# Squares moved to GpSimd, a first chunk in quarters, a last product in halves: one change to a two-layer hybrid block

## The chip, the cores and the metric

One core of one Trainium2 chip runs the whole program. The metric is the device time of one execution in microseconds (us); the median of several runs counts. The engines are TensorE (PE, its weight loads PEld), VectorE (DVE), ScalarE (ACT), GpSimd (POOL) and SyncE (SP), which issues nearly all DMAs here.

## What is computed

Two layers act on x of 256 tokens by 2048 features, float32. The first layer mixes a retention branch and a sparse attention branch, the second a convolution branch and a dilated attention branch. Each begins with a root-mean-square norm and a wide projection, and ends with an output product that is added to x:

```
def rms_norm(x, gain):
    y = x * rsqrt(mean(x * x, axis=-1) + 1e-6)
    return y * gain

def even_layer(x, ...):
    h = rms_norm(x, norm_g) @ w_in          # 2048 x 7704
    ...                                     # retention, sparse attention, gates
    return x + concatenate([a_out, b_out], -1) @ w_out

def odd_layer(x, ...):
    h = rms_norm(x, norm_g) @ w_in          # 2048 x 8192
    ...                                     # convolution, dilated attention, gates
    return x + concatenate([c_out, d_out], -1) @ w_out
```

The change touches the sum of squares and the first two projections at the very start, and the last output product at the very end.

## The kernel before

The kernel computes the products with three matmuls each: a float32 operand is split into a rounded part and a remainder, and hi x hi, hi x lo and lo x hi are added in PSUM. For weights the parts are `wh` (a cast on ScalarE, L109) and `wl` (`raw` minus `wh` on VectorE, L110), made by `prep`; a chunk of 512 rows of a weight comes in two halves of two k-tiles (128 rows) each, 128x1024 numbers a half. The pools of `raw`, `wh` and `wl` have five buffers each, so a load waits for a `wl` made earlier, and a cast for matmuls that are through with an earlier half. For x the parts are `xh` (ScalarE, L191) and `xl` (VectorE, L192), made by `norm_block` from `xT`, the transposed input, with the norm's gain multiplied in; the norm's factor per token is applied to the results later.

At the start `project_both` (L246) runs two projections side by side over four chunks c of x: for each c first the product into `mm` (q = 0), then that into `both` (q = 1). In the first chunk of q = 0 each k-tile is loaded, cast and split by itself (`cut`), with the load of the x k-tile between; all other chunks go by halves. `square_block` (L196) squares one block of four k-tiles of x on ScalarE (L201) and folds it on VectorE (L202, then L204 or L206, and L207) into `sqs`; `token_squares` (L213) sums that over the partitions on TensorE, and `token_rstd` makes the norm's factor with a power on GpSimd (L221). GpSimd has nothing but small settings of memory before that. `xtok` (L742), x by tokens for the residual sum, is loaded by SP into the place of `xT`, so its load waits until all reads of `xT` are done.

A planner in the compiler puts each engine's instructions into one fixed order by priority and estimated times; `high_priority` lifts weights and evacuations. In a run each engine keeps its order and waits on semaphores. So the order in which the engines work is not always that of the source lines.

At the end `project` (L114) computes the last output product, four times 512 columns: per chunk and half, for both token tiles t, six matmuls of 512 columns each. After a token tile's last matmul `evac_out` (L959) adds the residual on VectorE (L965) and stores (L966); for the very last tile it does so in two halves of 256 columns, one after the other.

Of the kernel before, what the change touches and what calls it, by code (L numbers as in the profile page):

```python
# [16 lines left out]
AF = mybir.ActivationFunctionType  # L17
ALU = mybir.AluOpType
# [18 lines left out]
HPO = 2000  # L37
# [22 lines left out]
def hybrid_kernel(ctx: ExitStack, tc: tile.TileContext, a: dict, out: bass.AP):  # L60
    nc = tc.nc
# [28 lines left out]
    def prep(src, n, cut=None, half=None):  # L90

        with tc.high_priority(offset=HPO):
            parts = []
            for hf in range(2):
                raw = wp.tile([128, 2, 512], F32, name="raw", tag="raw")
                wh = wp.tile([128, 2, 512], F32R, name="wh", tag="wh")
                wl = wp.tile([128, 2, 512], F32R, name="wl", tag="wl")
                if cut:
                    for k in range(2):
                        nc.sync.dma_start(raw[:, k, :n], src[:, 2 * hf + k, :])  # L100
                        cut(2 * hf + k)
                else:
                    nc.sync.dma_start(raw[:, :, :n], src[:, 2 * hf:2 * hf + 2, :])
                    if half:
                        half(hf)
                for k in ((0, 1), (1, 2)) if cut else ((0, 2),):
                    k = slice(*k)
                    r = raw[:, k, :n]
                    nc.scalar.copy(wh[:, k, :n], r)  # L109
                    nc.vector.tensor_sub(wl[:, k, :n], r, wh[:, k, :n].bitcast(F32))  # L110
                parts.append((wh, wl))
        return parts

    def project(src, n, lhs, evac, korder=None, lazy=None, extra=None, cut=None,  # L114
                flip=False):

        nch = src.shape[0]
        acc = [ps.tile([128, 512], F32, name=f"mm{t}", tag="mm", bufs=MMB) for t in range(2)]  # L120
        order = korder or list(range(nch))
        for i, c in enumerate(order):
            if lazy:
                lazy(c)
            parts = prep(src[c], n, cut=(lambda k: cut(c, k)) if cut and i < 3 else None)
            xh, xl = lhs[c]
            for hf in range(2):
                wh, wl = parts[hf]
                for t in range(2):
                    for j in range(2):  # L130
                        for k in range(2):
                            kk = 2 * hf + k
                            first = i == 0 and kk == 0
                            last = i == nch - 1 and kk == 3
                            if flip:
                                cs = slice((2 * t + j) * 128, (2 * t + j) * 128 + 128)
                                o = acc[t][:, j * S:j * S + S]
                                kw = dict(skip_group_check=True)
                                nc.tensor.matmul(o, wh[:, k, cs], xh[:, kk, :], start=first and j == 0, stop=False, **kw)  # L139
                                nc.tensor.matmul(o, wl[:, k, cs], xh[:, kk, :], start=False, stop=False, **kw)  # L140
                                nc.tensor.matmul(o, wh[:, k, cs], xl[:, kk, :], start=False, stop=last, **kw)  # L141
                            elif j == 0:
                                ts = slice(t * 128, t * 128 + 128)
                                o = acc[t][:, :n]
                                nc.tensor.matmul(o, xh[:, kk, ts], wh[:, k, :n], start=first, stop=False)  # L145
                                nc.tensor.matmul(o, xh[:, kk, ts], wl[:, k, :n], start=False, stop=False)  # L146
                                nc.tensor.matmul(o, xl[:, kk, ts], wh[:, k, :n], start=False, stop=last)  # L147
                    if i == nch - 1 and hf == 1:
                        with tc.high_priority(offset=HPO):
                            evac(t, acc[t])  # L150
            for f in (extra or {}).get(i, ()):
                f()
# [26 lines left out]
    xT = res.tile([128, KT, S], F32, name="xT", tag="x")  # L179
    sqs = [None]  # L180
# [14 lines left out]

    def square_block(b):  # L196

        if b == 0:
            sqs[0] = hp.tile([128, S], F32, name="sqs", tag="h")
        sq = hp.tile([128, 4, S], F32, name="sqb", tag="h")  # L200
        nc.scalar.activation(sq, xT[:, 4 * b:4 * b + 4, :], AF.Square)  # L201
        nc.vector.tensor_add(sq[:, 0:2, :], sq[:, 0:2, :], sq[:, 2:4, :])  # L202
        if b == 0:
            nc.vector.tensor_add(sqs[0], sq[:, 0, :], sq[:, 1, :])  # L204
        else:
            nc.vector.tensor_add(sq[:, 0, :], sq[:, 0, :], sq[:, 1, :])  # L206
            nc.vector.tensor_add(sqs[0], sqs[0], sq[:, 0, :])  # L207

    def token_squares(tot):

# [27 lines left out]
    lhs = []  # L238
# [4 lines left out]
    def load_x(b, k0=0, k1=4):  # L243
        nc.sync.dma_start(xT[:, 4 * b + k0:4 * b + k1, :], a["xT"][:, 4 * b + k0:4 * b + k1, :])

    def project_both(srcs, accs, evacs):  # L246

        nch = srcs[0].shape[0]
        for c in range(nch):
            for q in range(2):  # L250
                begin = c == 0 and q == 0
                parts = prep(srcs[q][c], 512, cut=(lambda k: load_x(0, k, k + 1)) if begin else None,
                             half=(lambda hf: load_x(c, 2 * hf, 2 * hf + 2)) if c and q == 0 else None)
                with tc.high_priority(offset=HPO):
                    if begin:
                        lhs.append(norm_block(0, evn, first=True))
                    elif q == 0:
                        lhs.append(norm_block(c, evn))
                if q == 0 and c == nch - 1:
                    square_block(c)  # L260
                xh, xl = lhs[c]
                for hf in range(2):
                    if q == 0 and c == nch - 1 and hf == 1:
                        rstd.append(token_rstd(token_squares(sqs[0]), "rstd1"))
                    wh, wl = parts[hf]
                    for t, k in [(t, k) for k in range(2) for t in range(2)] if begin else \
                            [(t, k) for t in range(2) for k in range(2)]:
                        kk = 2 * hf + k
                        last = c == nch - 1 and kk == 3
                        ts = slice(t * 128, t * 128 + 128)  # L270
                        o = accs[q][t]
                        nc.tensor.matmul(o, xh[:, kk, ts], wh[:, k, :], start=c == 0 and kk == 0, stop=False)  # L272
                        nc.tensor.matmul(o, xh[:, kk, ts], wl[:, k, :], start=False, stop=False)  # L273
                        nc.tensor.matmul(o, xl[:, kk, ts], wh[:, k, :], start=False, stop=last)  # L274
                        if last:
                            with tc.high_priority(offset=HPO):
                                evacs[q](t, o)
                if q == 0 and c < nch - 1:
                    square_block(c)
# [64 lines left out]
    for i, pos in enumerate((posk, posv)):  # L344
# [7 lines left out]
        for c in range(2):  # L352
            b = hp.tile([128, 16, 64], F32R, name=f"bhl{i}{c}", tag="h")
            nc.gpsimd.memset(b.bitcast(F32), 0.0)
            v = blk[:, 16 * c:16 * c + 16, :]
# [125 lines left out]
    for i in range(2):  # L481
        h = htile(f"nq{i}")
        if i == 0:
            def evac_gates(t, p, h=h):
# [4 lines left out]
                    extra={0: [k_turned, compress(1, 1)], 1: [k_normed], 2: [k_done, v_turned], 3: [v_done]})  # L489
# [14 lines left out]
    for h in range(8):  # L504
        for t in range(2):
            o = pc[:, (t * 8 + h) * 32:(t * 8 + h) * 32 + 32]
            k = kcT[:, h // 4, :, :].rearrange("p a n -> p (a n)")
# [26 lines left out]
    for h in range(8):  # L534
        g, r = h // 4, slice(32 * (h % 4), 32 * (h % 4) + 32)
        for n, src in enumerate((pch, pch, pcl)):
            v = src[r].rearrange("p (t g) k -> p t g k", t=2)[:, :, g, :]
# [137 lines left out]
    for hf in range(2):  # L675
# [5 lines left out]
        v = htile(f"rv{hf}")  # L681
# [55 lines left out]
    lhs = mix  # L737
# [3 lines left out]
    xtok = res.tile([128, 2, D], F32, name="xtok", tag="x")  # L741
# [29 lines left out]
    lhs = nxt  # L771
# [46 lines left out]
    apad, acc = [], []  # L818
# [77 lines left out]
    for p_ in range(3):  # L896
        v = htile(f"dv{p_}")
# [51 lines left out]
    mix, turns = [], []  # L949
    for i in range(3):  # L950
        extra = take(range(4))
# [5 lines left out]
    lhs = mix  # L957

    def evac_out(n):  # L959
        def f(t, p):  # L960
            w = 256 if n == 3 and t else 512
            for c in range(0, 512, w):
                k = 512 * n + c
                v = xtok[:, t, k:k + w]
                nc.vector.tensor_add(v, p[:, c:c + w], v)  # L965
                nc.sync.dma_start(out[t, :, k:k + w], v)  # L966
        return f

    for n in range(4):
        project(a["owo"][n], 512, lhs, evac_out(n), extra={} if n else {0: [turns[2]]})  # L970


def _constants():
# [87 lines left out]
```

## Time and profile before

| | |
|---|---|
| median of 3 runs | 939.23 us (939.16 to 939.35) |
| the profiled execution | 939.11 us |
| its span | 937.3 us |
| TensorE busy | 930.5 us (99%) |
| VectorE busy | 642.3 us (69%) |
| ScalarE busy | 507.5 us (54%) |
| GpSimd busy | 71.1 us (8%) |
| granted clock of TensorE | 0.999 of full speed |

The profile is one execution; its times count from the start of the span, and 1.8 us of the measured time lie around the span. In the chain of work that ended last TensorE has 97%. A mean over the span says little about the two places that the change touches, so the rows below are of these places, and of places where the engines in question worked side by side in a comparable way.

### The profile page before, as it was taken

Reading aid. Unit: us, or ns where it says so; the run is one execution under the profiler, and the core shown is the slowest. Engines: PE = TensorE matmul, PEld = TensorE weight load, DVE = VectorE, ACT = ScalarE, POOL = GpSimd, SP = SyncE. Lnnn points to the kernel's source line nnn. Section 1 sums busy time; section 2 is a strip of 40 time slices with the busy share of each in tenths; the row PEclk is TensorE's granted clock in tenths of the full one; section 3 lists DMA queues with packets and bytes.
Section 4 is the critical chain, followed back from the end, with each engine's and each line's share of the span. In section 5 each row is a group of like instructions: output and inputs, shape, how many; then the busy total and the mean of one; then the engine's idle time right before and its main releaser. Section 6 shows DMA issues by size and latency. Waiting matters only on the chain.

```text
span 937.3 us, 13151 instructions
## 1 busy us (share of the span) xinstructions
PE 930.5 (99%) x4949; PEld 798.7 (85%) x4949; DVE 642.3 (69%) x947; ACT 507.5 (54%) x762; POOL 71.1 (8%) x72
## 2 busy tenths in 40 slices
PE   8999999999999999999999999999999999999998
PEld 7889989989998888888888888888888888888886
DVE  7687657875654564654464499999999998546552
ACT  7566656655544544544465353556665444797341
POOL 0111100320220100000000000000000002200000
PEclk9999999999999999999999999999999999999999
DMA  9967754354446555555555555555555656434461
GB/s 332 348 204 220 249 189 149 120 176 156 152 164 207 161 170 182 185 195 181 196 185 168 192 180 180 190 190 190 185 186 185 202 197 189 148 116 157 149 226 53
DMA packets 52512, 173.48 MB, mean 185 GB/s; under 512 B 5728, under 2 KB 10720, under 8 KB 52320
## 3 DMA queue, kind: packets, MB, share of 16 engines
q1 hardware_dynamic: 52304, 172.63, 55.8%
q8 instruction: 39, 0.64, 0.3%
q14 instruction: 25, 0.20, 0.1%
q10 hardware_dynamic: 144, 0.01, 0.0%
HBM read 170.52 MB, written 2.10 MB: 184 GB/s over the span
## 4 chain that ended last, share of the span: by engine, by line
PE 97%; DMA 1%; DVE 1%; ACT 0%; issue 0%; SPq 0%; DVEq 0%
PE mm L145 25%; PE mm L147 25%; PE mm L146 25%; PE mm L139 3%; PE mm L141 3%; PE mm L140 3%; PE tr L315 3%; DMA raw<-in_ew 1%; PE dpo L931 1%; PE dsc L911 1%; PE cmph L377 1%; PE tr L579 1%; PE both L273 1%; PE both L274 0%; PE both L272 0%; PE mm L274 0%
## 5 line engine op out<-in xcount | busy, mean ns | idle before, releaser
L110 DVE TENSOR_TENSOR wl<-raw,wh 128x1024 fp32r<-128x1024 f32 (+2 forms) x322 | 385.1, 1202 | 215.0 <-ACT wh L109 208.1
L109 ACT CAST wh<-raw 128x1024 fp32r<-128x1024 f32 (+2 forms) x322 | 328.4, 1025 | 343.5 <-PE mm L147 252.1
L146 PE MATMUL mm<-wl,xh 128*128 128x512 f32 (+1 forms) x1056 | 406.4, 385 | 0.0
L145 PE MATMUL mm<-wh,xh 128*128 128x512 f32 (+1 forms) x1056 | 406.1, 386 | 0.0
L147 PE MATMUL mm<-wh,xl 128*128 128x512 f32 (+1 forms) x1056 | 403.3, 384 | 0.0
L147 PEld LDWEIGHTS mm<-wh,xl 128*128 128x128 f32 x1056 | 198.4, 188 | 38.1
L145 PEld LDWEIGHTS mm<-wh,xh 128*128 128x128 f32 x1056 | 198.2, 188 | 37.9 <-issue 0.2
L146 PEld LDWEIGHTS mm<-wl,xh 128*128 128x128 f32 x1056 | 198.5, 188 | 37.4
L801 DVE SCALAR_TENSOR_TENSOR cps<-apad,pb,cps 128x256 f32<-128x256 f32 x240 | 116.8, 487 | 5.3
L139 PE MATMUL mm<-xh,wh 128*128 128x256 f32 x256 | 73.2, 287 | 0.0
L140 PE MATMUL mm<-xh,wl 128*128 128x256 f32 x256 | 72.8, 285 | 0.0
L141 PE MATMUL mm<-xl,wh 128*128 128x256 f32 x256 | 72.5, 283 | 0.0
L140 PEld LDWEIGHTS mm<-xh,wl 128*128 128x128 f32 x256 | 49.0, 192 | 0.0
L141 PEld LDWEIGHTS mm<-xl,wh 128*128 128x128 f32 x256 | 49.0, 191 | 0.0
L139 PEld LDWEIGHTS mm<-xh,wh 128*128 128x128 f32 x256 | 48.9, 191 | 0.0
L567 ACT ACTIVATE p<-p,nm 128x128 f32<-128x128 f32 (+1 forms) x32 | 14.2, 445 | 15.5 <-DVE nm L563 15.4
L643 POOL TENSOR_TENSOR rot<-rot,pb 128x512 f32<-128x512 f32 x8 | 11.2, 1406 | 78.3 <-ACT rot L641 78.0
L299 ACT ACTIVATE sq<-d 128x128 f32<-128x128 f32 x48 | 14.3, 303 | 0.3
L273 PE MATMUL both<-wl,xh 128*128 128x512 f32 x32 | 12.8, 401 | 1.2 <-DVE wl L110 1.2
L644 POOL TENSOR_TENSOR rT<-rT,rot 128x512 f32<-128x512 f32 x8 | 13.1, 1660 | 0.0
L272 PE MATMUL both<-wh,xh 128*128 128x512 f32 x32 | 12.6, 394 | 0.0
L274 PE MATMUL both<-wh,xl 128*128 128x512 f32 x32 | 12.5, 390 | 0.0
(294 smaller groups left out, 724.0 us busy)
## 6 DMA issues: line engine op xcount, KB each, us to landing
raw<-in_ow SPq DMA_DIRECT2D x128, 512.0 KB, 4.5
raw<-in_ew SPq DMA_DIRECT2D x110, 512.0 KB, 4.2
raw<-in_ewo SPq DMA_DIRECT2D x32, 512.0 KB, 4.0
raw<-in_owo SPq DMA_DIRECT2D x24, 512.0 KB, 4.1
raw<-in_ewn SPq DMA_DIRECT2D x16, 268.0 KB, 3.5
xtok<-in_xtok SPq DMA_DIRECT2D x1, 2048.0 KB, 8.3
raw<-in_w1k SPq DMA_DIRECT2D x4, 512.0 KB, 6.4
raw<-in_w1v SPq DMA_DIRECT2D x4, 512.0 KB, 4.2
```

Source lines behind the costliest of these rows:

```text
L109: nc.scalar.copy(wh[:, k, :n], r)
L110: nc.vector.tensor_sub(wl[:, k, :n], r, wh[:, k, :n].bitcast(F32))
L139: nc.tensor.matmul(o, wh[:, k, cs], xh[:, kk, :], start=first and j == 0, stop=False, **kw)
L140: nc.tensor.matmul(o, wl[:, k, cs], xh[:, kk, :], start=False, stop=False, **kw)
L141: nc.tensor.matmul(o, wh[:, k, cs], xl[:, kk, :], start=False, stop=last, **kw)
L145: nc.tensor.matmul(o, xh[:, kk, ts], wh[:, k, :n], start=first, stop=False)
L146: nc.tensor.matmul(o, xh[:, kk, ts], wl[:, k, :n], start=False, stop=False)
L147: nc.tensor.matmul(o, xl[:, kk, ts], wh[:, k, :n], start=False, stop=last)
L273: nc.tensor.matmul(o, xh[:, kk, ts], wl[:, k, :], start=False, stop=False)
L299: nc.scalar.activation(sqv[:, t, h, :], view[:, t, h, :], AF.Square, accum_out=ss[:, t * nh + h:t * nh + h + 1])
L315: nc.tensor.transpose(pt[:, i * 128:(i + 1) * 128], b, ident)
L801: nc.vector.scalar_tensor_tensor(p, src, w, p, op0=ALU.mult, op1=ALU.add)
```

## The change

Three parts. The squares of blocks 0 to 2 of x, and their sums, go from ScalarE and VectorE to GpSimd; those of block 3 stay, and its last sum on VectorE now adds to what GpSimd has left in `sqs`. The first chunk of the second projection is loaded, cast and split by k-tiles, like that of the first; the x of k-tiles 2 and 3 comes in one load in place of two. In the last product the very last six matmuls become twelve of 256 columns, in the order of the column halves, and each half is added and stored when it ends.

```diff
@@ project
+                    split_ = tail and t == 1 and i == nch - 1 and hf == 1
+                    if split_:
+                        for j in range(2):
+                            o, js = acc[t][:, j * 256:j * 256 + 256], slice(j * 256, j * 256 + 256)
+                            for k in range(2):
+                                kk, ts = 2 * hf + k, slice(128, 256)
+                                kw = dict(start=False, skip_group_check=True)
+                                nc.tensor.matmul(o, xh[:, kk, ts], wh[:, k, js], stop=True, **kw)
+                                nc.tensor.matmul(o, xh[:, kk, ts], wl[:, k, js], stop=True, **kw)
+                                nc.tensor.matmul(o, xl[:, kk, ts], wh[:, k, js], stop=True, **kw)
+                            with tc.high_priority(offset=HPO):
+                                evac(t, acc[t], j)
+                        continue
...
-                            last = i == nch - 1 and kk == 3
+                            last = i == nch - 1 and kk == 3 or tail and t == 1 and i == nch - 1 and kk == 1
@@ square_block
-        nc.scalar.activation(sq, xT[:, 4 * b:4 * b + 4, :], AF.Square)
+        x = xT[:, 4 * b:4 * b + 4, :]
+        if b < 3:
+            nc.gpsimd.tensor_tensor(sq, x, x, op=ALU.mult)
+            nc.gpsimd.tensor_add(sq[:, 0:2, :], sq[:, 0:2, :], sq[:, 2:4, :])
+            if b == 0:
+                nc.gpsimd.tensor_add(sqs[0], sq[:, 0, :], sq[:, 1, :])
+            else:
+                nc.gpsimd.tensor_add(sq[:, 0, :], sq[:, 0, :], sq[:, 1, :])
+                nc.gpsimd.tensor_add(sqs[0], sqs[0], sq[:, 0, :])
+            return
+        nc.scalar.activation(sq, x, AF.Square)
         nc.vector.tensor_add(sq[:, 0:2, :], sq[:, 0:2, :], sq[:, 2:4, :])
-        if b == 0:
-            nc.vector.tensor_add(sqs[0], sq[:, 0, :], sq[:, 1, :])
-        else:
-            nc.vector.tensor_add(sq[:, 0, :], sq[:, 0, :], sq[:, 1, :])
-            nc.vector.tensor_add(sqs[0], sqs[0], sq[:, 0, :])
+        nc.vector.tensor_add(sq[:, 0, :], sq[:, 0, :], sq[:, 1, :])
+        nc.vector.tensor_add(sqs[0], sqs[0], sq[:, 0, :])
@@ project_both
+        def load_first(k):
+            if k < 2:
+                load_x(0, k, k + 1)
+            elif k == 2:
+                load_x(0, 2, 4)
...
-                parts = prep(srcs[q][c], 512, cut=(lambda k: load_x(0, k, k + 1)) if begin else None,
+                parts = prep(srcs[q][c], 512, cut=(load_first if q == 0 else lambda k: None) if c == 0 else None,
@@ evac_out
-        def f(t, p):
-            w = 256 if n == 3 and t else 512
-            for c in range(0, 512, w):
-                k = 512 * n + c
-                v = xtok[:, t, k:k + w]
-                nc.vector.tensor_add(v, p[:, c:c + w], v)
-                nc.sync.dma_start(out[t, :, k:k + w], v)
+        def f(t, p, j=None):
+            c, w = (0, 512) if j is None else (256 * j, 256)
+            v = xtok[:, t, 512 * n + c:512 * n + c + w]
+            nc.vector.tensor_add(v, p[:, c:c + w], v)
+            nc.sync.dma_start(out[t, :, 512 * n + c:512 * n + c + w], v)
...
-        project(a["owo"][n], 512, lhs, evac_out(n), extra={} if n else {0: [turns[2]]})
+        project(a["owo"][n], 512, lhs, evac_out(n), extra={} if n else {0: [turns[2]]}, tail=n == 3)
```

## Rows read from the trace of the kernel before

**Rows 1.** Waits of TensorE, whole span: total us, times, longest us

```profile
PE both L273 <- DVE wl L110: 1.2, 2, 0.9
```

**Rows 2.** Timeline of TensorE: start us, us, what, idle before and its releaser

```profile
11.34 0.50 PE L272 MATMUL both<-wh,xh 128*128 128x512 f32 x1
...
12.71 0.50 PE L273 MATMUL both<-wl,xh 128*128 128x512 f32 x1 [0.87 <-DVE wl L110]
...
27.40 0.50 PE L273 MATMUL both<-wl,xh 128*128 128x512 f32 x1 [0.30 <-DVE wl L110]
```

**Rows 3.** Busy us by engine in one stretch, then clock, DMA share, GB/s

```profile
18.00:27.00 9.00, 9.00 (x41) 7.17 (x39) 8.96 (x19) 9.00 (x15) 0.00 (x0) 1.00 0.99 365
```

**Rows 4.** Timeline of VectorE, 8 to 28 us

```profile
8.35 0.48 DVE L192 SCALAR_TENSOR_TENSOR xl<-xT,evn,xh 128x256 fp32r<-128x256 f32 x1
9.02 0.69 DVE L110 TENSOR_TENSOR wl<-raw,wh 128x512 fp32r<-128x512 f32 x1 [0.19 <-ACT wh L109]
9.63 0.48 DVE L192 SCALAR_TENSOR_TENSOR xl<-xT,evn,xh 128x256 fp32r<-128x256 f32 x1
...
23.27 1.27 DVE L192 SCALAR_TENSOR_TENSOR xl<-xT,evn,xh 128x256 fp32r<-128x256 f32 x3
...
26.13 1.22 DVE L110 TENSOR_TENSOR wl<-raw,wh 128x1024 fp32r<-128x1024 f32 x1
```

**Rows 5.** Instructions of the squares' tile: ns min/median/max, first and last start

```profile
L201 ACT ACTIVATE sqb<-xT x4: 1043/1046/1048, 9.3 to 23.4; 128x1024 f32<-128x1024 f32 x4
L202 DVE TENSOR_TENSOR sqb<-sqb x4: 683/684/692, 10.4 to 25.2; 128x512 f32<-128x512 f32 x4
L206 DVE TENSOR_TENSOR sqb<-sqb x3: 418/420/425, 19.3 to 27.3; 128x256 f32<-128x256 f32 x3
L207 DVE TENSOR_TENSOR sqs<-sqs,sqb x3: 418/419/419, 21.1 to 29.9; 128x256 f32<-128x256 f32 x3
```

**Rows 6.** Timeline of GpSimd and of VectorE, 787 to 797 us

```profile
789.12 2.40 POOL L847 TENSOR_TENSOR chsum<-acc,acc 128x1024 f32<-128x1024 f32 x1 [71.41 <-ACT acc L813]
791.61 2.16 POOL L848 TENSOR_TENSOR chsum<-chsum 128x512 f32<-128x512 f32 x1
...
790.50 2.11 DVE L110 TENSOR_TENSOR wl<-raw,wh 128x1024 fp32r<-128x1024 f32 x1 [1.43 <-ACT wh L109]
```

**Rows 7.** Timeline of GpSimd, 806 to 808 us

```profile
806.21 1.28 POOL L848 TENSOR_TENSOR chsum<-chsum 128x512 f32<-128x512 f32 x1
807.58 0.73 POOL L849 TENSOR_TENSOR chsum<-chsum 128x256 f32<-128x256 f32 x1
```

**Rows 8.** Timeline of GpSimd and of VectorE, 247 to 250 us

```profile
247.12 2.74 POOL L643 TENSOR_TENSOR rot<-rot,pb 128x512 f32<-128x512 f32 x2 [50.28 <-ACT rot L641]
...
247.13 0.69 DVE L642 TENSOR_TENSOR rT<-mm,pb 128x512 f32<-128x512 f32 x1 [0.36 <-ACT rot L641]
```

**Rows 9.** Timeline of GpSimd and of VectorE, 62 to 66 us

```profile
62.62 2.84 POOL L171 TENSOR_SCALAR kn0rsm<-kn0ss 128x4 f32<-128x4 f32 x1 [21.85 <-DVE kn0ss L303]
...
63.03 2.37 DVE L110 TENSOR_TENSOR wl<-raw,wh 128x1024 fp32r<-128x1024 f32 x2
```

**Rows 10.** Timeline of SP's DMA issues, 25 to 33 us

```profile
25.35 0.33 SPq L742 DMA_DIRECT2D xtok<-in_xtok  x1
27.37 5.54 SPq L103 DMA_DIRECT2D raw<-in_ew  x5
```

**Rows 11.** The last matmul, the last adds, and the stores of L966

```profile
933.11 0.39 PE L147 MATMUL mm<-wh,xl 128*128 128x512 f32 x1
933.53 0.76 DVE L965 TENSOR_TENSOR xtok<-mm,xtok 128x256 f32<-128x256 f32 x2 [0.67 <-PE mm L147]
L966 SPq DMA_DIRECT2D out<-xtok x9: 332/343/384, 888.5 to 934.4; - x9
```

**Rows 12.** Timeline of TensorE, matmuls of 256 columns, 266.8 to 267.0 us

```profile
266.84 0.28 PE L141 MATMUL mm<-xl,wh 128*128 128x256 f32 x1
266.96 0.28 PE L139 MATMUL mm<-xh,wh 128*128 128x256 f32 x1
```

More of the change, by code (lines that the diff above doesn't have):

```diff
@@ L114, in project @@
     def project(src, n, lhs, evac, korder=None, lazy=None, extra=None, cut=None,
-                flip=False):
+                flip=False, tail=False):
         nch = src.shape[0]
```

## The prediction

> **What bounds the kernel now.** I read four views in this order: waits of TensorE over the whole span, the table of stretches for the first 36 us, the timeline of VectorE there, and the last 5 us.
>
> The waits of TensorE come first. After the opening matmuls they name one releaser only, VectorE's `wl` of L110, 1.2 us in all [rows 1]; its two places in the timeline are 12.71 and 27.40 us [rows 2]. From 27.40 to the last product TensorE waits for nothing. So a change can take time from this kernel only ahead of 27.40 us or behind the last matmul, and any time that TensorE loses anywhere is added to the end, one for one.
>
> The table of stretches shows what stands behind the second wait. From 18 to 27 us VectorE is busy 8.96 of 9.00 us [rows 3]: it is full there, and TensorE with 41 matmuls in 9.00 us (0.22 us each) goes just as fast as VectorE feeds it. In VectorE's timeline the `wl` that TensorE waits for at 27.40 starts at 26.13 and ends at 27.35, and `xl` of two blocks and the squares' sums stand ahead of it [rows 4]. The first part of the change touches just this queue.
>
> **The squares.** Removed: three Squares of 1.04 us from ScalarE, and from VectorE three L202 of 0.68 us and five sums of 0.42 us (L206 and L207 twice each, and L204 of the same form) [rows 5], in all 3 x 0.68 + 5 x 0.42 = 4.1 us, all of it ahead of 26.13. If nothing took its place, both waits of rows 2 could go: at 12.71 `both` has run only one matmul since 11.34, so 12.71 - 11.34 - 0.22 = 1.15 us, and at 27.40 0.30 us, together 1.45 us.
>
> Added, on GpSimd: a product of 128x1024, a sum of 128x512, and one (block 0) or two (blocks 1, 2) sums of 128x256. The nearest rows are the channel sums of the convolution, the same forms: 2.40 us for 128x1024 [rows 6], 1.28 and 0.73 us for the smaller two, when VectorE leaves them alone [rows 7]. Block 0 costs 2.40 + 1.28 + 0.73 = 4.41 us, blocks 1 and 2 5.14 us each, 14.7 us in all. GpSimd's own queue has nothing else there, so by itself this would be hidden.
>
> It isn't by itself. Rows 6 show what GpSimd's sums do to `wl`. The 128x1024 sum ran from 789.12 to 791.52; the `wl` that was issued beside it at 790.50 took 2.11 us in place of 1.22 [rows 4], and ended at 792.61, just 1.09 us after the sum. The sum that followed was issued at 791.61 and took 2.16 us in place of 1.28: it ended 1.16 us behind that `wl`. They did not share; each stood still until the other was through, turn by turn. An operation of VectorE that reads PSUM goes on undisturbed: L642 took 0.69 us beside a GpSimd product [rows 8]. All of VectorE's work in the first 30 us is of the first kind, with two operands in SBUF: `wl` from `raw` and `wh`, `xl` from `xT` and `xh`.
>
> The Trainium skill, page "SBUF — State Buffer", section "Who interferes with whom", states this as a rule: a VectorE instruction with two SBUF inputs and a GpSimd instruction that reads SBUF exclude each other, and whichever is second waits until the first has finished. By that rule the trace agrees for `wl` (2.11 beside 1.22 us), and `xl` would be in it too; no row here shows an `xl` beside GpSimd.
>
> I take `xl` as `wl`, since it too reads two tiles in SBUF; that it is free is a rival below. So VectorE gives up 4.1 us and is put behind up to 14.7 us. The sum goes to the same place where TensorE waits now, the end of `wl` at 27.35. From 8.35 us, when the first block's `x` is about to be complete, VectorE still has to do up to there: five `wl` of 128x512 at 0.61 us (9.02 to 9.63 in rows 4; one for the last k-tile of the first projection and, new, four for the second's first chunk), four of 128x1024 at 1.18 (two in 2.37 [rows 9]), fourteen `xl` at 0.42 (three in 1.27), and one L202 at 0.61: 3.05 + 4.72 + 5.88 + 0.61 = 14.3 us. With GpSimd's 14.7 us in turn between them that is 29.0 us, and 8.35 + 29.0 = 37.35 in place of 27.35: **+10.0 us**. As VectorE has 24 instructions there and GpSimd 11, turns one by one let GpSimd finish its eleven before that `wl`. Afterwards VectorE is free again and is ahead of TensorE as before, but TensorE, which never waits later, can't get the time back.
>
> Bounds. Above: the pair may also stand idle, when GpSimd has finished block 0 and block 1's `x` is not there yet; I allow 2 us, an estimate from the 1.15 us wait that loads leave now, so +12. Below: if block 2 (5.14 us) fell behind that `wl`, +4.9; if the order on VectorE put `wl` ahead of the eight `xl` of blocks 2 and 3 (8 x 0.42 = 3.4 us), +6.6. I take +10.0, the sum for the order as it stands. Two further waits are added: SP's load of `xtok` overwrites `xT` and now waits for GpSimd's product of block 2 as well, with the loads of the following chunk behind it on SP (25.35 and 27.37 us now [rows 10]); and VectorE's last L207 waits for GpSimd's sums. In turns, block 2's product would end about 25 us, so the first adds little.
>
> **The second projection's first chunk by k-tiles.** Loads, casts and `wl` come in quarters, so the first `wl` could be ready about half a `wl` and half a cast earlier. Alone it is worth at most the 1.15 us at 12.71, and it would be given back at 27.40, because VectorE sets that point: nothing of it comes in front of a full queue. VectorE pays 4 x 0.61 - 2 x 1.18 = 0.08 us, within the sum. SP issues two more weight loads and one `x` load fewer, each about 0.33 us [rows 10]; joining `x` of k-tiles 2 and 3 makes k-tile 2 wait for twice the bytes. I cost both at nothing: the first chunk is then held by GpSimd's first product anyway. Without that cover it would be 0.3 us either way.
>
> **The last product by halves.** Today the last matmul starts at 933.11, VectorE adds two halves from 933.53 to 934.29, and the last store is issued at 934.4 [rows 11]. Afterwards the six last matmuls are twelve of 256 columns. Such matmuls, each with its own weights, stand 0.12 us apart [rows 12]: 12 x 0.12 = 1.44 in place of 6 x 0.22 = 1.32 us, +0.1 us. The first half's add then falls beside the second half's matmuls, so one add of 0.38 us leaves the end: **-0.3 us**. Bounds: -0.4 (matmuls cost nothing more) to +0.1 (the end hangs on the store's landing only).
>
> **Sum.** Profiled execution 939.11 us (span 937.3 and 1.8 around it) + 10.0 - 0.3 = 948.8. The median of the runs is 939.23, 0.1 above it, so **948.9 us**.
>
> **Rivals.**
>
> *Turns as forecast*, chance 0.55: 948.9, own range 943.5 to 951.5 by the bounds above.
>
> *VectorE keeps the pair while it has work*, 0.12. For it: a tiny GpSimd operation issued at 62.62 took 2.84 us, to 65.46, just past two `wl` that ran one after the other till 65.40 [rows 9]. Against it: it was that instruction's first use, which may cost time by itself. Then 27.40 moves little, but GpSimd's products pile up behind VectorE's queue, which in rows 4 is full up to 27.35. Block 2's product would end near 27 + 12 = 39 us (14.7 less its last three sums, 2.7), and `xtok` with the loads behind it moves from 25.35 by about 13.6. TensorE comes to that data at 27.40 + 60 x 0.22 = 40.6, 13.2 us after their issue today; what of that is slack no row says, so the loss is 0.4 to 13.6. I take the middle, 7: 946.
>
> *Only `wl` collides, `xl` does not*, 0.13. For it: `xl` is another form (SCALAR_TENSOR_TENSOR) and no row shows it beside GpSimd. Then GpSimd's time lies beside the 5.88 us of `xl`: 29.0 - 5.9 = 23.1, so 31.5 in place of 27.35, +4.1: 943.0.
>
> *The other side: GpSimd's squares hold the pair only briefly*, 0.14. The rows of collision are sums of two tiles; a product of a tile with itself, and sums in place, might keep VectorE out for less than they last. It decides at 4.1 us, the work that VectorE is rid of: if it is kept out for less than 4.1 of the 14.7 us (28%), `wl` comes earlier than today. If for none, both waits go: -1.45 - 0.3 = -1.75, or 937.4; the opening wait ahead of 12.71 [rows 2] might shrink too, to 937.0. Against it stand rows 6 and 7: both later sums there are in place, and kept `wl` waiting or waited for it.
>
> *The change does not do what it says*, 0.06: the compiler's planner puts GpSimd's work or the quarters elsewhere, and gain and loss cancel near 939 to 941.
>
> **Chances.** A measurement of this kernel can tell about 0.2% (1.9 us) from no change. Slower by more than that: turns 0.55, VectorE keeps 0.12, only `wl` 0.13, together 0.80. Faster by more: 0.08 of the other side's 0.14, since 937.4 lies right at the bound of 937.35. Within: its other 0.06 and the last rival's 0.06, 0.12. The range 939.0 to 952.0 leaves out the other side (0.14) and about 0.04 above; its upper end is the +12 bound and 0.8 us for a TensorE that waits longer than any row shows.
>
> **What would show it.** Right: GpSimd's 128x1024 product at about 8 us and, beside it, `wl` and `xl` of two to three times their 0.69 and 0.48 us; GpSimd's own sums longer than 1.28 and 0.73; TensorE's waits of together some 10 us ahead of 40 us, nearly all put down to `wl` and `xl`; none later; the last store issued about 0.3 us sooner after the last matmul. `xl` at 0.48 beside a GpSimd product speaks for the third case, `wl` at 1.22 beside it for the other side, long products that end only after 35 us for the second. The forecast is wrong if VectorE's instructions keep their lengths while GpSimd works.

## The result, and the profile after

| | before | changed |
|---|---|---|
| median of 4 runs each | 939.19 us | 944.75 us (944.11 to 945.36) |
| ratio, 95% interval | | 1.0060 (1.0048 to 1.0072) |
| profiled execution, its span | 939.11, 937.3 us | 944.45, 942.6 us |

The changed kernel is slower by 5.6 us, 0.6%. The sign, the place and the mechanism are those of the forecast (948.9 us); the loss is little more than half of the 9.7 us forecast. The time goes with the mean granted clock of TensorE: two of the four runs, at 1.000, took 944.11 and 944.45 us, the two at 0.998 and 0.996 took 945.04 and 945.36. In the changed kernel `wl` is L110, `xl` L206, the opening matmuls L301 to L303, the squares on GpSimd L218 to L224.

The waits of TensorE over the whole span come first again (total us, times, longest us), for the changed kernel, the opening `xh` and `cold` (warm-up matmuls on a constant tile at the very start) left out. They answer to [rows 1]:

```profile
PE mm L302 <- DVE wl L110: 1.9, 3, 1.1
PE both L302 <- DVE wl L110: 1.4, 2, 0.7
PE mm L303 <- DVE xl L206: 1.0, 1, 1.0
...
PE mm L138 <- DVE xtok L992: 0.5, 1, 0.5
```

Where there was 1.2 us of waits for `wl`, there are 3.3 us, and a wait for `xl` that did not exist. New and not foreseen is the wait for `xtok` in the last product (L138).

The table of stretches (length, then busy us and count of PE, PEld, DVE, ACT and POOL, clock, DMA share, GB/s) for the kernel before, and then for the changed one; [rows 3] is the stretch between the two:

```profile
5.00:18.00 13.00, 11.71 (x48) 8.79 (x49) 10.88 (x17) 10.45 (x16) 0.00 (x0) 1.00 1.00 364
27.00:36.00 9.00, 8.70 (x41) 7.17 (x41) 5.72 (x8) 2.13 (x3) 0.00 (x0) 1.00 0.93 355
```

```profile
5.00:18.00 13.00, 10.43 (x41) 7.19 (x42) 11.73 (x14) 9.39 (x16) 6.62 (x4) 1.00 0.96 314
18.00:27.00 9.00, 8.21 (x34) 5.71 (x32) 9.00 (x6) 7.43 (x13) 8.92 (x7) 1.00 0.93 349
27.00:36.00 9.00, 7.48 (x30) 5.54 (x31) 8.96 (x15) 4.20 (x4) 1.69 (x2) 1.00 0.59 188
```

The counts of matmuls tell more than the busy time: TensorE is 7, 7 and 11 behind in the three stretches. Four of the 25 are the small sums of the squares, which both kernels run but the changed one only at 37.67 us; the other 21 are 4.8 us at 0.227 us each. VectorE in the middle stretch is as full as before, 9.00 of 9.00 us, but with 6 instructions where there were 19 [rows 3]: it is busy by the record and stands still for most of it.

That standing still is visible in the timelines of GpSimd and of VectorE (start us, us, what, count), changed kernel, 8 to 33 us:

```profile
8.34 2.25 POOL L218 TENSOR_TENSOR sqb<-xT 128x1024 f32<-128x1024 f32 x1 [5.41 <-DMA xT<-in_xT]
...
20.15 2.07 POOL L218 TENSOR_TENSOR sqb<-xT 128x1024 f32<-128x1024 f32 x1
22.18 1.71 POOL L223 TENSOR_TENSOR sqb<-sqb 128x256 f32<-128x256 f32 x1
...
27.96 0.81 POOL L224 TENSOR_TENSOR sqs<-sqs,sqb 128x256 f32<-128x256 f32 x1
```

```profile
8.76 3.56 DVE L206 SCALAR_TENSOR_TENSOR xl<-xT,evn,xh 128x256 fp32r<-128x256 f32 x2
12.23 4.75 DVE L110 TENSOR_TENSOR wl<-raw,wh 128x512 fp32r<-128x512 f32 x6
...
16.91 3.55 DVE L206 SCALAR_TENSOR_TENSOR xl<-xT,evn,xh 128x256 fp32r<-128x256 f32 x2
20.38 2.91 DVE L110 TENSOR_TENSOR wl<-raw,wh 128x1024 fp32r<-128x1024 f32 x1
23.22 2.38 DVE L206 SCALAR_TENSOR_TENSOR xl<-xT,evn,xh 128x256 fp32r<-128x256 f32 x2
25.53 1.76 DVE L110 TENSOR_TENSOR wl<-raw,wh 128x1024 fp32r<-128x1024 f32 x1
27.21 2.64 DVE L206 SCALAR_TENSOR_TENSOR xl<-xT,evn,xh 128x256 fp32r<-128x256 f32 x4
29.77 1.22 DVE L110 TENSOR_TENSOR wl<-raw,wh 128x1024 fp32r<-128x1024 f32 x1
30.90 1.66 DVE L206 SCALAR_TENSOR_TENSOR xl<-xT,evn,xh 128x256 fp32r<-128x256 f32 x4
```

The `wl` issued at 20.38 lies beside GpSimd's product of 20.15 to 22.22 and takes 2.91 us, 1.22 when alone (29.77). GpSimd's next sum, issued at 22.18, then takes 1.71 us where such a sum takes 0.73 [rows 7]. A pair of `xl` takes 3.56 us in place of 0.87 (four in 1.66 at 30.90, so 0.48 and 0.39 for a pair). The two engines take turns, and `xl` is in it as `wl` is.

The end of that chain in TensorE's timeline, changed kernel, and then a row of the kernel before; the row of 31.04 is the matmul that stands at 27.40 in [rows 2]:

```profile
31.04 0.50 PE L302 MATMUL both<-wl,xh 128*128 128x512 f32 x1 [0.69 <-DVE wl L110]
...
33.70 0.61 PE L301 MATMUL mm<-wh,xh 128*128 128x512 f32 x2
34.82 0.50 PE L302 MATMUL mm<-wl,xh 128*128 128x512 f32 x1 [0.50 <-DVE wl L110]
```

```profile
26.49 0.61 PE L272 MATMUL mm<-wh,xh 128*128 128x512 f32 x2
```

It is 31.04 - 27.40 = 3.64 us late there, and at the last six wide matmuls' place 5.01 us: they started at 933.11 - 5 x 0.227 = 931.97 us [rows 11], the changed block starts at 936.98. Of the 1.4 us between, 2 x 0.227 = 0.45 us are not a later loss: the two matmuls of 33.70 had been run ahead of the wait in the kernel before (26.49), so TensorE was really 4.1 us behind at 31.04. The wait at 34.82 adds 34.82 - 33.70 - 0.45 = 0.67 us, and restarts some 0.2 us more.

The last product, VectorE and TensorE, answering to [rows 11]:

```profile
937.18 1.14 DVE L992 TENSOR_TENSOR xtok<-mm,xtok 128x512 f32<-128x512 f32 x2 [6.53 <-PE mm L161]
937.57 0.28 PE L140 MATMUL mm<-wh,xl 128*128 128x256 f32 x1
938.37 0.39 PE L138 MATMUL mm<-wh,xh 128*128 128x256 f32 x1 [0.52 <-DVE xtok L992]
...
939.38 0.42 DVE L992 TENSOR_TENSOR xtok<-mm,xtok 128x256 f32<-128x256 f32 x1 [1.07 <-PE mm L140]
```

The row of 937.18 holds the add of the other token tile and then the first half's add, to 938.32. The second half's matmuls don't run beside that add; they start when it has ended, at 938.37. From the start of the block to the last add's end it is 939.80 - 936.98 = 2.82 us, before 934.29 - 931.97 = 2.32: +0.5 us in this execution, not -0.3.

### The profile page after: what moved, and what is told of

Read it like the earlier page. It is cut to its first block, busy times and chain, and to the rows that moved or that the text cites. A ratio compares the mean times of both kernels' runs of the same rounds, so it can differ in the third digit from the quotient of the medians.

```text
span 942.6 us, 13170 instructions
## 1 busy us (share of the span) xinstructions
PE 933.0 (99%) x4955; PEld 799.1 (85%) x4955; DVE 649.3 (69%) x941; ACT 506.7 (54%) x761; POOL 88.3 (9%) x83
## 4 chain that ended last, share of the span: by engine, by line
PE 96%; DMA 2%; DVE 1%; issue 0%; SPq 0%; DVEq 0%
PE mm L159 25%; PE mm L161 25%; PE mm L160 25%; PE mm L153 3%; PE mm L154 3%; PE mm L155 3%; PE tr L344 3%; DMA raw<-in_ew 1%; PE dpo L960 1%; PE dsc L940 1%; DMA xT<-in_xT 1%; PE cmph L406 1%; PE tr L608 1%; DVE wl L110 1%; DVE xl L206 1%; PE mm L302 0%
## 5 line engine op out<-in xcount | busy, mean ns | idle before, releaser
L110 DVE TENSOR_TENSOR wl<-raw,wh 128x1024 fp32r<-128x1024 f32 (+2 forms) x324 | 388.0, 1205 | 215.2 <-ACT wh L109 209.6
L206 DVE SCALAR_TENSOR_TENSOR xl<-xT,evn,xh 128x256 fp32r<-128x256 f32 x16 | 14.8, 967 | 0.0
L302 PE MATMUL mm<-wl,xh 128*128 128x512 f32 x32 | 12.1, 404 | 1.9 <-DVE wl L110 1.9
```

The costliest lines, as they stand in the source:

```text
L206: nc.vector.scalar_tensor_tensor(xl[:, k, :], x, g, xh[:, k, :].bitcast(F32), op0=ALU.mult, op1=ALU.subtract)
```

## The experiments

The theory: GpSimd's squares, which read SBUF, and VectorE's instructions with two SBUF operands keep each other waiting, turn by turn, and `wl` and `xl` reach TensorE late; the other two parts matter little. The rivals to be told apart: that a busy GpSimd, or the squares' absence from ScalarE and VectorE, or the new order of VectorE's work does it; that only a few of GpSimd's instructions count; and that the quarters or the halves cost the time. Each ratio is against the kernel before on the same chip (its medians 938.9 us).

**The squares alone** (`sq_only`): the diff of `square_block`, nothing else.

```diff
+        if b < 3:
+            nc.gpsimd.tensor_tensor(sq, x, x, op=ALU.mult)
+            nc.gpsimd.tensor_add(sq[:, 0:2, :], sq[:, 0:2, :], sq[:, 2:4, :])
...
+            return
```

> The kernel before with the squares of blocks 0 to 2 on GpSimd and neither of the other two parts. Theory (GpSimd's sums and VectorE's wl and xl exclude each other): nearly all of the front's loss of 5.0 us is here, so 4 to 6.5 us above before, with xl of 1.5 to 2.1 us beside GpSimd's products. Rival (the loss comes from the first chunk by quarters, from the joined x load or from the other order of VectorE): within 1 us of before.

Measured: 946.78 us, ratio 1.0084 (1.0069 to 1.0100), 7.8 us slower, more than the 4 to 6.5 us expected; this part makes the whole loss, and alone it makes more of it than in company. First its waits of TensorE, then VectorE's and TensorE's timelines, then a table of stretches:

```profile
PE both L281 <- DVE wl L110: 4.3, 3, 2.8
```

```profile
26.63 4.21 DVE L192 SCALAR_TENSOR_TENSOR xl<-xT,evn,xh 128x256 fp32r<-128x256 f32 x8
30.76 0.68 DVE L213 TENSOR_TENSOR sqb<-sqb 128x512 f32<-128x512 f32 x1
...
31.82 2.35 DVE L110 TENSOR_TENSOR wl<-raw,wh 128x1024 fp32r<-128x1024 f32 x2
```

```profile
33.09 0.50 PE L281 MATMUL both<-wl,xh 128*128 128x512 f32 x1 [2.84 <-DVE wl L110]
...
35.31 0.63 PE L281 MATMUL both<-wl,xh 128*128 128x512 f32 x1
35.74 0.63 PE L282 MATMUL both<-wh,xl 128*128 128x512 f32 x1
```

```profile
30.00:33.00 3.00, 0.25 (x2) 0.00 (x0) 2.97 (x7) 1.04 (x1) 0.00 (x0) 1.00 0.38 82
...
35.00:37.00 2.00, 2.00 (x6) 1.53 (x5) 2.00 (x3) 0.00 (x0) 0.00 (x0) 0.50 0.99 414
```

Here all eight `xl` of blocks 2 and 3 and two sums of block 3 stand ahead of the `wl` for which TensorE waits, as the forecast had the `xl`. The matmul of 27.40 comes at 33.09, 5.7 us late. And after the wait of 2.84 us the granted clock falls to 0.50 for some 3.4 us (33.7 to 37.1): matmuls stand 0.43 us apart (35.31, 35.74) in place of 0.227, eight of them, so about 8 x 0.2 = 1.6 us more. 5.7 + 1.6 = 7.3 us, as the spans differ (944.6 - 937.3); the medians differ by 7.8.

**GpSimd as busy, but not reading** (`sq_memset`): blocks 0 to 2 get constants in place of their squares' sums, so the norm's factor isn't the reference's.

```diff
+            nc.gpsimd.tensor_copy(sq[:, 0, 0:1], x[:, 0, 0:1])
+            nc.gpsimd.tensor_copy(sq[:, 3, 0:1], x[:, 3, 0:1])
+            for _ in range(5):
+                nc.gpsimd.memset(sq, 1.0)
+            if b == 0:
+                nc.gpsimd.memset(sqs[0], 2048.0)
```

> As sq_only, but GpSimd's product and sums of each block are replaced by two copies of one column and five memsets of 128x1024 (0.96 us each as in the kernel before, about 14 us in all), which write SBUF and read next to nothing of it. The sums of squares of blocks 0 to 2 are left out, constants stand in their place, so the norm's factor is another. Theory (what excludes VectorE is GpSimd reading SBUF): wl and xl keep 1.22 and 0.48 us, TensorE's front waits go, 0.5 to 2 us below before. Rival (a busy GpSimd as such, or the changed order of VectorE and the relieved ScalarE, makes the loss): 4 us or more above before, like sq_only.

Measured: 938.98 us, ratio 0.9999 (0.9990 to 1.0008). GpSimd's and VectorE's timelines:

```profile
18.63 1.22 POOL L204 COPY sqb<-xT 128x1 f32<-128x1 f32 x1
...
20.97 6.71 POOL L207 MEMSET sqb<- 128x1024 f32 x7
```

```profile
12.01 3.80 DVE L110 TENSOR_TENSOR wl<-raw,wh 128x1024 fp32r<-128x1024 f32 x3 [1.93 <-ACT wh L109]
...
18.58 1.23 DVE L110 TENSOR_TENSOR wl<-raw,wh 128x1024 fp32r<-128x1024 f32 x1
19.72 3.25 DVE L192 SCALAR_TENSOR_TENSOR xl<-xT,evn,xh 128x256 fp32r<-128x256 f32 x8
```

GpSimd is as busy (8.83 us of the stretch 18 to 27, 8.92 in the changed kernel), ScalarE and VectorE are rid of the same work, and `wl` and `xl` keep their lengths, 1.23 us and 3.25 / 8 = 0.41 us. The loss of 7.8 us is gone. So it is the reading of SBUF by GpSimd that costs it. The one-column copy says the same by itself: issued at 18.63, just behind the `wl` of 18.58, it reads only 128x1 numbers and yet ends at 19.85, when that `wl` has ended (19.81), while a MEMSET of 128x1024 beside `wl` keeps its 0.96 us. That the kernel is not below the one before, though VectorE has 4.1 us less to do, is a miss of the theory (0.5 to 2 us below): in the stretch from 5 to 18 us it has 46 matmuls against 48. TensorE waits 0.58 us for a cast at 12.03 and then 0.76 us for the `wl` behind that cast, for which VectorE itself sat idle 1.93 us. So the first of the two waits of [rows 2] stays when the squares leave VectorE; the second is gone. What delays the cast was not followed further.

**One block of three** (`sq_one`): as `sq_only`, with `b < 1`.

> The kernel before with the squares of block 0 alone on GpSimd (no other part). Theory (VectorE is put behind by about what GpSimd's instructions last, here 2.0 + 1.3 + 0.7 = 4.0 us, less the 1.1 us of its own that it gives up): 1.5 to 3.0 us above before. Rival (the loss comes when GpSimd works beside the fullest stretch, 18 to 27 us, and block 0, done by 13 us, is hidden): within 0.7 us of before.

Measured: 941.26 us, ratio 1.0021 (1.0012 to 1.0031), 2.4 us slower: by the median within the theory's 1.5 to 3.0 us. VectorE's timeline beside GpSimd's product of 8.33 to 10.41 us:

```profile
8.58 2.37 DVE L110 TENSOR_TENSOR wl<-raw,wh 128x512 fp32r<-128x512 f32 x1
10.87 1.50 DVE L192 SCALAR_TENSOR_TENSOR xl<-xT,evn,xh 128x256 fp32r<-128x256 f32 x1
```

Alone such a `wl` takes 0.69 and such an `xl` 0.48 us [rows 4]. VectorE was not yet full there, and time is lost all the same, since TensorE waits for these parts of the first chunk. The size is less certain than the median says. Three of the ten runs, the profiled one among them, have a mean granted clock of 0.999 or 1.000 and took 939.7 to 939.9 us, 0.8 to 1.0 above the kernel before; the other seven, at 0.997 or 0.998, took 941.0 to 942.2 us. No trace of these seven was kept. So the turns alone are seen to cost about 0.9 us here, less than the theory said and just more than its rival's 0.7; the rest of the 2.4 us goes with the lower clock.

**The quarters alone** (`kt_only`): the diff of `project_both`; and **with x in four loads** (`kt_x4`):

```diff
+        def load_first(k):
+            load_x(0, k, k + 1)      # kt_only: k = 2 loads 2 and 3 together
...
+                parts = prep(srcs[q][c], 512, cut=(load_first if q == 0 else lambda k: None) if c == 0 else None,
```

> The kernel before with only the first chunk of the second projection by k-tiles and the joined x load. By the prediction it is worth nothing, since VectorE's full queue ahead of 27.40 us takes it back: within 0.5 us of before. Rival: the wait at 12.71 us goes and stays gone, 1.1 us below before.

> As kt_only (first chunk of the second projection by k-tiles, squares as before), but with x of the first block in four loads. Theory: kt_only gained the 1.15 us wait at 12.71 and lost 1.2 us by the joined x load, so without the joining 0.5 to 1.2 us below before. The prediction's view (VectorE's full queue ahead of 27.40 gives the gain back): within 0.4 us of before, with a wait for wl of 1 us or more near 26 us.

Measured: `kt_only` 938.64 us, ratio 0.9995 (0.9986 to 1.0004); `kt_x4` 937.73 us, 0.9988 (0.9979 to 0.9997). `kt_only`, timelines of ScalarE and of TensorE:

```profile
9.32 0.91 ACT L191 ACTIVATE xh<-xT,evn 128x256 fp32r<-128x256 f32 x2 [1.52 <-DMA xT<-in_xT]
```

```profile
9.88 0.73 PE L279 MATMUL mm<-wh,xh 128*128 128x512 f32 x2 [1.21 <-ACT xh L191]
```

`kt_x4`, timelines of TensorE and of VectorE:

```profile
12.40 0.50 PE L277 MATMUL both<-wl,xh 128*128 128x512 f32 x1 [0.21 <-DVE wl L110]
```

```profile
24.52 1.21 DVE L110 TENSOR_TENSOR wl<-raw,wh 128x1024 fp32r<-128x1024 f32 x1
25.65 0.87 DVE L192 SCALAR_TENSOR_TENSOR xl<-xT,evn,xh 128x256 fp32r<-128x256 f32 x2
```

Part 2 is nothing on the whole, but of two sizes that cancel. The joined load holds k-tile 2 until both k-tiles have landed, and TensorE waits 1.21 us for it. With four loads the quarters bring 1.2 us by the medians: the 0.87 us wait of [rows 2] is 0.21. Nothing of it is given back later, since the planner now puts two of block 3's `xl` behind the `wl` that stood last in [rows 4] (25.65 after 24.52), and that one is ready at 25.73, not 27.35. The profiled execution of `kt_x4`, 938.38 us, is among the slower of its eleven (937.26 to 938.79) and waits 1.00 us for an `xh` at 7.51, so its rows show less than the median's gain.

**The squares where VectorE has room** (`kt_gate`): part 2, with all squares on ScalarE and VectorE as before, but those of blocks 0 to 2 issued later. The Square gets a bias of zero made from the `wl` in question, so it can't start sooner. VectorE's order up to that `wl` is then instruction for instruction that of the changed kernel.

```diff
-        nc.scalar.activation(sq, xT[:, 4 * b:4 * b + 4, :], AF.Square)
+        nc.scalar.activation(sq, xT[:, 4 * b:4 * b + 4, :], AF.Square, bias=zero[0])
...
+                if q == 1 and c == 1:
+                    z = const.tile([128, 1], F32, name="sqz")
+                    nc.vector.tensor_scalar(z, parts[1][1][:, 0, 0:1].bitcast(F32), 0.0, None, op0=ALU.mult)
+                    zero[0] = z
+                    square_block(0)
+                    square_block(1)
+                if q == 0 and c == 2:
+                    square_block(2)
```

> Squares stay on ScalarE and VectorE, but those of all blocks wait (through a zero bias made from a wl) until the wl of the second chunk of the second projection is done; first chunk by k-tiles. VectorE then has the same instructions in the same order up to that wl as in the changed kernel, without GpSimd beside it. Theory (what the front lost is GpSimd's exclusion and nothing else): both of TensorE's waits on wl go, 1.0 to 1.8 us below before and 6 to 7 below the changed kernel. Rival (loads or ScalarE set these points): within 0.5 us of before.

Measured: 937.60 us, ratio 0.9986 (0.9977 to 0.9995), 1.3 us below the kernel before, as expected, and 7.2 below the changed one. VectorE's timeline, and below it the longest of TensorE's waits after the opening matmuls:

```profile
21.45 1.23 DVE L110 TENSOR_TENSOR wl<-raw,wh 128x1024 fp32r<-128x1024 f32 x1 [0.64 <-ACT wh L109]
```

```profile
PE mm L279 <- ACT xh L191: 0.9, 1, 0.9
```

In the same place of the same order that `wl` ends at 22.68 us, in the changed kernel at 30.99. Neither the order nor the missing squares explain a loss; GpSimd beside VectorE does. The wait for `xh` is the joined load again.

**The same with x in four loads** (`gate_x4`): `kt_gate` and `kt_x4` together.

> As kt_gate, but with x of the first block in four loads, as in the kernel before. In kt_gate TensorE still waits 0.9 us for xh of k-tile 2, whose x came in the joined load (1.2 us in kt_only). Theory (the joined load makes k-tile 2 wait for twice the bytes): that wait goes, 0.4 to 1.0 us below kt_gate, 936.6 to 937.2 us. Rival (the first 9 us are bound by the bytes of all loads together, whatever their cut): within 0.3 us of kt_gate.

Measured: **936.87 us**, ratio 0.9977 (0.9967 to 0.9986): 2.0 us below the kernel before, 7.9 below the changed one, and 0.7 below `kt_gate`, within the 0.4 to 1.0 expected of the unjoined load. All of TensorE's waits in it:

```profile
PE cold L165 <- DVE heat L162: 1.0, 1, 1.0
PE mm L276 <- DVE xh L189: 0.2, 1, 0.2
```

**The halves alone** (`tail_only`): the diff of `project` and `evac_out`. And **with both adds behind the twelve matmuls** (`tail_behind`), as the kernel before has it:

```diff
-                            with tc.high_priority(offset=HPO):
-                                evac(t, acc[t], j)
+                        with tc.high_priority(offset=HPO):
+                            evac(t, acc[t], 0)
+                            evac(t, acc[t], 1)
```

> The kernel before with only the last product by halves. The prediction's term: 0.3 us below before, the first half's add beside the second half's matmuls. Theory from the changed kernel's trace: the second half's matmuls wait 0.5 us for the first half's add, because both halves lie in one PSUM tile; the last add then ends 0.3 to 0.5 us later than before, 0.2 to 0.4 us above before.

> As tail_only with the twelve matmuls of 256 columns, but both adds and both stores behind the last matmul, so that no matmul follows an add. It measures the price of the narrow matmuls alone: twelve at 0.12 us for six at 0.227, last matmul's start later by 0.1 to 0.2 us, time 0.0 to 0.2 us above before. If the narrow matmuls themselves made the tail longer (rival), it would be as late as tail_only.

Measured: `tail_only` 939.30 us, ratio 1.0002 (0.9994 to 1.0011); `tail_behind` 938.97 us, 0.9999 (0.9990 to 1.0008). Neither differs from the kernel before by its runs; the profiled executions, one each, show the parts. `tail_only`, TensorE and VectorE:

```profile
933.51 0.39 PE L138 MATMUL mm<-wh,xh 128*128 128x256 f32 x1 [0.52 <-DVE xtok L977]
934.53 0.42 DVE L977 TENSOR_TENSOR xtok<-mm,xtok 128x256 f32<-128x256 f32 x1 [1.07 <-PE mm L140]
```

`tail_behind`, the last matmul and the adds:

```profile
932.37 0.28 PE L140 MATMUL mm<-wh,xl 128*128 128x256 f32 x1
932.68 0.76 DVE L978 TENSOR_TENSOR xtok<-mm,xtok 128x256 f32<-128x256 f32 x2 [0.74 <-PE mm L140]
```

From the block's first matmul to the last add's end: 2.32 us before, 933.44 - 931.05 = 2.39 with both adds behind, 934.95 - 932.13 = 2.82 with the first between. Twelve narrow matmuls cost 0.07 us, as forecast (0.1); the add between them costs 0.43 more where 0.4 less was forecast.

## Why the forecast was right, and where it was wrong

**The mechanism and its place: right.** GpSimd's instructions that read SBUF and VectorE's with two SBUF operands take turns (20.38 and 22.18 above), a GpSimd that only writes costs nothing (`sq_memset`), and the loss is made ahead of 36 us. The Trainium skill, page "SBUF — State Buffer", section "Who interferes with whom", says that the contention is with a GpSimd instruction that reads SBUF, and not with one that only writes it; the two experiments agree, `wl` 2.91 us beside the product (`sq_only`) and 1.23 beside MEMSET (`sq_memset`).

**The rivals fall.** "Only `wl` collides": `xl` takes up to 2.12 us beside GpSimd in the changed kernel and 1.50 in `sq_one`, 0.48 alone. "VectorE keeps the pair" (the pair is what the two engines take in turns): GpSimd ends at 28.77 us, not near 39, and SP's issue of `xtok`, moved from 25.35 to 32.71 us, is no wait of TensorE. "The other side": VectorE would have had to be kept out for less than 4.1 us; it was 10.6. "Doesn't do what it says": GpSimd runs just what the source says.

**The sum: the path right, two terms too large.** The forecast put the end of the deciding `wl` at 37.35 us; it was 30.99.

- *How long GpSimd keeps VectorE out.* Forecast 14.7 us, the recorded lengths of eleven instructions. Measured by VectorE's rows, each against its length alone: 2.69 (8.76) + 0.53 (the first of the six at 12.23, 1.21 us) + 2.68 (16.91) + 1.69 (20.38) + 1.51 (23.22) + 0.54 (25.53) + 0.98 (27.21) = 10.6 us. So 4.1 us too many. A product of a tile with itself takes 1.94 to 2.08 us in `sq_only` where the row taken for it, a sum of two tiles, took 2.40 [rows 6]: three times about 0.4, 1.2 us. The remaining 2.9 us are 0.26 us for each of eleven turns, in which GpSimd's record runs and VectorE is not held. [rows 6] had it already: `wl` ended 1.09 us after the sum, not its full 1.22, and the next sum 1.16 us after that `wl`, not 1.28. These 0.13 and 0.12 us are saved at each turn; the forecast read the rows as standing still and summed full lengths. What a GpSimd instruction does in these 0.26 us was not tested.
- *What stands ahead of that `wl`.* The forecast kept the order of before and named the other as a bound (+6.6, `wl` ahead of eight `xl`). The planner took a way between: four `xl` of block 3 (30.90) and block 3's first sum stand behind `wl` now, 4 x 0.42 + 0.61 = 2.3 us. 37.35 - 4.1 - 2.3 = 30.95. In `sq_only`, where the order is nearly that of the forecast (one sum more stands ahead), TensorE starts again at 33.09: 37.35 - 4.1 = 33.25.
- *"Afterwards VectorE is ahead of TensorE as before": wrong.* The four `xl` and the two sums that stand behind that `wl` stand ahead of the next, which TensorE waits for at 34.82. That wait and the restarts brought back some 0.9 us: TensorE was 4.1 us behind at 31.04, counting the two matmuls that it had not yet run, and 5.01 at the end.
- *"Both waits could go" when the squares leave VectorE: half wrong.* In `sq_memset` only the wait of 27.40 goes; one like that of 12.71 stays, behind the cast (0.76 us at 13.29). So the 1.45 us, and with them the 937.4 us of "the other side", were too much: `sq_memset`, the nearest to that case, took 938.98 us.

**The quarters: right at nothing for part 2 alone, by luck.** Two sizes that the forecast had wrong cancel. "Given back at 27.40" failed; the quarters keep 1.2 us (`kt_x4`, by its interval 0.3 to 2.0). "Joining x: 0.3 us either way" failed; by the medians it costs 0.9 (938.64 against 937.73), and 0.7 beside the later squares (937.60 against 936.87). And in company part 2 was not nothing: with parts 2 and 3 the changed kernel is 2.0 us below `sq_only` (944.75 against 946.78). The traces show two differences that go that way: another order on VectorE, with four `xl` fewer ahead of the deciding `wl`, and with it no wait of 2.84 us and no fall of the clock, which cost about 1.6 us (all four runs of `sq_only` have a mean granted clock of 0.996 to 0.998). A run with the quarters and `sq_only`'s order was not made, so how the 2.0 us divide is not shown.

**The halves: a wait overlooked.** The forecast let the first half's add lie beside the second half's matmuls. Both halves lie in one PSUM tile, and the matmuls wait for the add (0.52 us at 938.37). So the restart is late by 938.37 - 937.57 - 0.12 = 0.68 us, against an add of 0.34 (0.76 - 0.42) that leaves the end. The Trainium skill, page "PSUM — Partial Sum Buffer", section "PSUM bank collisions raise a hardware error", says that TensorE's writes and VectorE's reads may not meet in one bank and set of partitions, even at other columns, so this wait could not simply be taken away; the trace agrees, in so far as no second-half matmul starts before the add has ended. Halves in two tiles were not tried.

**Together.** Forecast +10.0 - 0.3 = +9.7; in the profiled executions +5.0 at the front and +0.5 at the end, 5.5 against 942.6 - 937.3 = 5.3 us of span. What lies behind the last add made up the other 0.2 and was not followed. The medians differ by 5.6 us; the two runs at the lower clock are in that.

## What to carry to other kernels

Moving work to an idle engine is priced by what it keeps other engines from: eleven GpSimd instructions took 4.1 us from VectorE's queue and held it for 10.6, in the stretch where it fed TensorE. Where a queue is full, look first for when it has room; the same squares, on their old engines but later, and x in separate loads gave 936.87 us. And take no order of a planned queue for granted: here 2.3 us of VectorE's work stood on the other side of the deciding `wl` than forecast, so sum a forecast for the order at hand and for the nearest other.

## What the runs showed of the hardware that was not expected

- TensorE's granted clock fell to 0.50 (1.2 GHz) after one wait of 2.84 us, with 0.25 us of matmuls in the 3 us ahead of 33 us (`sq_only`), and was back at 37.1 us. Waits up to 1.1 us in the changed kernel's profiled execution left it at 1.00. So one long wait cost some 1.6 us beyond its own length. Runs with a mean clock of 0.998 or less exist of the kernel before too (three of 32, 940.7 to 940.9 us against 939.4 at most for the others); what lowered the clock in them no trace shows.
- GpSimd's product of a tile with itself (128x1024) took 1.94 to 2.08 us (`sq_only`), the sum of two such tiles 2.40 [rows 6].
- VectorE's `wl` and `xl` are not held for the whole recorded length of a GpSimd instruction beside them, but for some 0.26 us less; [rows 6] shows 0.25.
- A GpSimd copy that reads one column of SBUF waited for a whole `wl`: 1.22 us (`sq_memset`, 18.63), where the one issued at 20.69, behind an `xl` nearly done, took 0.35.
